# One list for all 48 weight-sum steps of the second FFN, two chains alternating, drawn on from the first FFN's last third

## The chip, the cores and the metric

The kernel runs on one core of a Trainium2 chip. The metric is the device time of one execution in microseconds, lower is better. Three executions of the kernel before took 1138.20, 1135.95 and 1139.35 us, with a median of 1138.2 us. For this kernel a difference under about 0.3% (3.4 us) cannot be told from no change.

## The reference

One decoder layer over 512 tokens of width 1024, in float32. Two feed-forward blocks (FFN, hidden width 2816) stand around a pair of parallel token mixers:

```python
h = x
h = h + 0.5 * swiglu(rmsnorm(h, norm_ffn1), ffn1_gate, ffn1_up, ffn1_down)
u = rmsnorm(h, norm_mix)
parts = split(u @ w_in)                       # queries, keys, values, gates of both mixers
o_a = native_sparse_attention(...)            # compressed + selected blocks + window of 512
o_b = sliding_window_attention(...)           # window of 128, with sinks
merged = sigmoid(ga) * (o_a @ w_branch_a) + sigmoid(gb) * (o_b @ w_branch_b)
h = h + merged @ w_out
h = h + 0.5 * swiglu(rmsnorm(h, norm_ffn2), ffn2_gate, ffn2_up, ffn2_down)
out = rmsnorm(h, norm_final)

def swiglu(x, w_gate, w_up, w_down):
    return (silu(x @ w_gate) * (x @ w_up)) @ w_down
```

## The kernel before, in words

**Products.** Every float32 weight block and every operand is split into a high and a low part, and a product is made of three matmuls (high x high, high x low, low x high). One weight block is 512 KB in most places (128 partitions x 1024 floats). Its way is: SP loads it into one of four `raw` buffers (L143), ACT casts the high part `whi` (L151), DVE subtracts to get the low part `wlo` (L155), and PE uses both. There are four `whi`/`wlo` slots. Casts are issued two blocks ahead of the matmuls that need them, and the load of block n + 4 goes into the buffer that the low part of block n has freed. SP carries these loads in program order.

**Fewer products by weight sums.** Some stages use a 2 x 2 block scheme with seven products in place of eight. It needs sums and differences of quarters of the weights. These are not made on an engine: POOL issues DMAs from HBM to HBM, of two kinds, a plain copy into a scratch tensor and an accumulating one that adds to it (`issue`, L396 to L401: L399 accumulates, L401 copies). A weight sum is a chain of eight such steps over four scratch tensors, where most steps need the one or two before them in the same chain to have landed, and POOL waits for that in its own queue before it issues the step. The first FFN has its own sums (`unit_sums`, tensors `s_...`, 32 steps of 512 KB; lines L478 and L480), for the tiles 8 to 15 of its hidden width ("unit" stage, matmuls at L791).

**The 48 steps of the second FFN**, 1 MB each, are six chains of eight:

- four chains from `four_steps(f)` for f = 0, 8, 12, 17 (`FOURS`): scratch tensors named `w`. Each serves 14 weight blocks (`raw<-w` and quarters of gate and up) of a tile group of four (function `four`, matmuls at L1883, 14 blocks of 12 matmuls each).
- two chains from `down_sums(f0)` for f0 = 0, 8: scratch tensors named `t`. They serve the first and the second down projection (function `down`).

The order in which the second FFN uses them: tiles 4, 5, then `four` 0, tiles 6, 7, first `down`; `four` 8, `four` 12, tile 16, second `down`; `four` 17, tile 21, and the last down projection.

**Who draws a step, before.** Three generators hold the 48 steps, and a `next(...)` written at some place of the program emits one step into POOL's queue at that place:

- `in_mixers` holds 24 steps, three chains in turn (`four` 0, `four` 8, `down` 0). `Schedule.follow` draws them at 24 places of the mixers' instruction list `ORDER`, which is written out by hand.
- `in_merge` holds the 8 steps of `four` 12, drawn at every second turn of the merge's two loops over d (the gated merge and the product with `w_out`).
- `in_ffn2` holds 16 steps, first the 8 of `down` 8, then the 8 of `four` 17, one chain after the other. They are drawn at places inside the second FFN.

A place in the program is only a place in POOL's queue. POOL issues a step as soon as what stands ahead of it in its queue is done and the step's own predecessors have landed, whatever PE does then.

**What else stands in POOL's queue** near these steps: in the first FFN's last third and in the merge, the running sum of squares `sqacc` for the next norm (L673); in the mixers low parts (L155), rotations (L1186, L1265) and the weighing of probabilities (L1582, L1584); in the merge the product of a stored gate with the norm's factor (`z<-z,r_b`, L1750).

Of the kernel before, what the change touches and what calls it, by code (L numbers as in the profile page):

```python
# [362 lines left out]
def layer(ctx, tc, a, out):  # L363
# [33 lines left out]
    def issue(o, i, add):  # L397
        if add:
            gpsimd.dma_start(o, i, accum_op=OP.add)  # L399
        else:  # L400
            gpsimd.dma_start(o, i)  # L401

    def down_sums(f0):

        def part(j, k):
            return dram(a["ffn2_down"], (f0 + j) * 128 * D + k * 512, [[D, 128], [256 * D, 4], [1, 512]])

        t = [t_sums[f0, k] for k in range(4)]
        return [(t[0], part(0, 1), 0), (t[2], part(0, 1), 0), (t[0], part(0, 0), 1), (t[2], part(1, 1), 1),
                (t[1], t[0], 0), (t[1], part(1, 1), 1), (t[3], t[1], 0), (t[3], part(1, 0), 1)]  # L410
# [3 lines left out]
    def four_steps(f):  # L414

        g0, g1, u0, u1 = (dram(a[f"ffn2_{what}"], kh * 512 * DFF + f * 128, [[DFF, 512], [1, 512]])
                          for what in ("gate", "up") for kh in range(2))
        t1, t3, t2, t4 = (four_sums[f, m] for m in (5, 7, 6, 4))
        return [(t1, g0, 0), (t3, u0, 0), (t1, u0, 1), (t3, u1, 1), (t2, t1, 0), (t2, u1, 1), (t4, t2, 0), (t4, g1, 1)]

    def in_mixers():

        x = [y for z in zip(four_steps(FOURS[0]), four_steps(FOURS[1]), down_sums(0)) for y in z]
        for y in x:
            issue(*y)
            yield

    def in_merge():

        for y in four_steps(FOURS[2]):  # L430
            issue(*y)
            yield

    def in_ffn2():

        for y in down_sums(8) + four_steps(FOURS[3]):
            issue(*y)
            yield

    def four_block(f, m, kk):  # L440

# [374 lines left out]
    def ffn(after, begun, side, sums, early):  # L816


        norm = {}

        def col():
            norm["col"] = col_of(sums)

        def rows():
            norm_rows(norm["col"])
            for j, b in enumerate(begun):
                swiglu(*b, j)

        lo, hi = UNITS[1]
        adds = unit_sums(1)  # L830
        for third, (f0, f1) in enumerate(THIRDS):
            f = f0 + (len(begun) if f0 == 0 else 0)
            while f < f1:
                if lo <= f < hi:
                    if f == lo:
                        W.full, W.more_bufs = len(W.raw) - 1, 0
                    unit(f - f0)
                    f += 2
                    if f > lo + 2:
                        next(early, None)  # L840
                    continue
                first = f == len(begun)
                pg = acc(False)
                mm3(pg, W.next(), u_in, KD, col if first else None)
                pu = acc(False)
                mm3(pu, W.next(), u_in, KD, rows if first else None)
                swiglu(pg, pu, f - f0)
                f += 1
                if third == 0:
                    if f == 8:  # L850
                        sums_of_u(0, 0)
                    next(side, None)
                    for _ in range(6):
                        next(adds, None)
                else:
                    next(early, None)
                    next(side, None)
            settle(later)
            settle(owed)
            for d in range(KD):  # L860
                po = acc(False)
                mm3(po, W.next(), g_in, f1 - f0)
                if third == 2 and d < KD - 1:
                    W.prep(W.pos + W.AHEAD)
                vector.scalar_tensor_tensor(h[:, d], po, 0.5, h[:, d], op0=OP.mult, op1=OP.add)
                if third == 0:
                    if d < 3:
                        sums_of_u(0, d + 1)
                    next(side, None)
                if third == 1 and d in (0, 2, 4, 6, 7):  # L870
                    next(early, None)
                if third == 2:
                    after(d)
        for g in (adds, side, early):
            for _ in g:
                pass
# [128 lines left out]
    with ExitStack() as mixing:  # L1005
# [693 lines left out]
        nsa_count, swa_turns = [0], []  # L1699
        attend([*swa_units(0), *swa_units(1), *nsa_units(0), *nsa_units(1, (3, 2, 1, 0))])  # L1700
        plan.clock["sp"] = plan.clock["store"] = 0.0
        plan.follow(ORDER, in_mixers())
        W.pos = pos[0]
        W.prepped = pos[0] + 2
        att_stack.close()
# [33 lines left out]
                stt(p[:, 1], y[:, :256], -1.0, p[:, 0], op0=OP.mult, op1=OP.subtract)  # L1739
            split(four_hi[:, k, 2 * second:2 * second + 2], four_lo[:, k, 2 * second:2 * second + 2], p)  # L1740

        merge_steps = in_merge()

        with pool("merge", 2, side="right") as mp:
            mh, ml = (mp.tile([128, KD, S], F32R, name=n, bufs=1) for n in ("mh", "ml"))

            def load_z(d):
                z = mp.tile([128, S], F32, name="z%d" % (d // KD))
                nc.sync.dma_start(z, zd[d])
                gpsimd.tensor_tensor(z, z, r_b, op=OP.mult)  # L1750
                return z

            za, zb = load_z(0), None
            for d in range(KD):
                nc.sync.dma_start(h[:, d], hd[d])
                gates_z = [za, zb]
                if d + 1 < KD:
                    za = load_z(d + 1)
                if d not in GB_EARLY:
                    gates_z[1] = mp.tile([128, S], F32, name="z1")  # L1760
                    ps = acc(False)
                    mm3(ps, W.next(), u_in, KD)
                    vector.tensor_tensor(gates_z[1], ps, r_b, op=OP.mult)
                if d + 1 in GB_EARLY:
                    zb = load_z(KD + d + 1)
                for z, x in zip(gates_z[::-1], (b_in, a_in)):
                    scalar.activation(z, z, AF.Sigmoid)
                    ps = acc(False)
                    mm3(ps.rearrange("p (t c) -> p t c", t=4), W.next(), x, 4)
                    vector.tensor_tensor(z, z, ps, op=OP.mult)  # L1770
                y, z = gates_z
                vector.tensor_tensor(y, y, z, op=OP.add)
                split(mh[:, d], ml[:, d], y)
                if d % 2 == 0:
                    next(merge_steps, None)

            m_in = (lambda k: mh[:, k]), (lambda k: ml[:, k])
            for d in range(KD):
                ps = acc(False)
                mm3(ps, W.next(), m_in, KD)  # L1780
                vector.tensor_tensor(h[:, d], ps, h[:, d], op=OP.add)
                norm_in(d, 2)
                for i in {4: (0, 1), 5: (2,), 6: (3,)}.get(d, ()):
                    sums_of_tokens(i, mp, ("z0", "z1"))
                if d % 2:
                    next(merge_steps, None)


    with pool("temp3", 2) as temp, pool("end") as end:
# [175 lines left out]
                for n in range(4):  # L1965
                    turns.append(lambda n=n: whole(n))

        turns, steps = [], in_ffn2()

        def turn_back():  # L1970
            if turns:
# [192 lines left out]
```

## Time and profile before

| | |
|---|---|
| median of three runs | 1138.2 us |
| the profiled execution | 1138.66 us |
| its span, first to last instruction | 1136.9 us |
| PE busy | 1096.1 us (96%) |
| DVE, ACT, POOL busy | 757.9, 541.5, 218.8 us |
| moved by POOL's DMA queue (q0) | 67.11 MB in 26176 packets |
| moved by SP's DMA queue (q1) | 159.98 MB in 172696 packets |

The stages, by the start of their matmuls: first FFN up to 366 us (unit stage 143 to 224 us), mixers up to about 640 us, merge and `w_out` up to 748 us, second FFN to the end. A row of the windows view gives, for a stretch of time, each engine's busy time with its count of instructions, the granted TensorE clock (1.00 is full), the mean busy share of the 16 DMA engines and the rate. In a timeline row the square bracket holds the idle time of the engine before the instruction and what ended it.

### The profile page before, as it was taken

How to read it: one execution, taken by the hardware profiler on the slowest of the kernel's cores; microseconds unless marked ns; L12 is line 12 of the kernel's file. 1: busy time of each engine (PE TensorE's matmuls, PEld its weight loads, DVE VectorE, ACT ScalarE, POOL GpSimd, SP SyncE). 2: the span in 40 equal slices, each digit the busy share in tenths (PEclk: the TensorE clock that was granted, in tenths of full speed). 3: DMA queues.
4: the chain of work that ended last, by engine and by line, in shares of the span. 5: the costliest groups of instructions: out<-in, count | busy, mean ns of one | idle time of the engine just before them, and what ended most of it. 6: DMA issues, size and time to landing. Idle time of an engine off the chain costs nothing.

```text
span 1136.9 us, 15814 instructions
## 1 busy us (share of the span) xinstructions
PE 1096.1 (96%) x5827; PEld 938.9 (83%) x5827; DVE 757.9 (67%) x1358; ACT 541.5 (48%) x988; POOL 218.8 (19%) x253
## 2 busy tenths in 40 slices
PE   9999999999999998999999999977959999999987
PEld 7888899988888998998888888866748888888876
DVE  5656777854556588987777376554647876787653
ACT  5433344432344466767677434435434446554432
POOL 0211210000003145744345322221100000000002
PEclk9999999999999999999999999989989999999999
DMA  6988979788756365359897879669996565646612
GB/s 210 260 214 211 241 186 263 228 286 259 246 179 176 86 186 161 116 170 262 268 236 253 217 239 259 170 157 264 297 257 194 193 196 167 187 148 196 212 56 75
DMA packets 201414, 232.44 MB, mean 204 GB/s; under 512 B 7924, under 2 KB 152120, under 8 KB 201016
## 3 DMA queue, kind: packets, MB, share of 16 engines
q1 hardware_dynamic: 172696, 159.98, 44.4%
q0 software_dynamic: 26176, 67.11, 25.6%
q10 hardware_dynamic: 2464, 4.33, 1.0%
q8 instruction: 46, 0.75, 0.3%
q14 instruction: 32, 0.26, 0.1%
HBM read 211.47 MB, written 87.03 MB: 263 GB/s over the span
## 4 chain that ended last, share of the span: by engine, by line
PE 82%; DVE 8%; DMA 4%; ACT 3%; issue 2%; POOL 0%; POOLq 0%; ACTq 0%; DVEq 0%; SPq 0%
PE acc L387 27%; PE o L387 19%; PE s L387 18%; PE o L791 3%; PE o L1883 3%; PE acc L1883 2%; PE s L1883 2%; DMA raw<-in_ffn_up_dram 2%; PE tp L1647 2%; PE s L791 2%; PE acc L791 2%; DVE wlo L155 2%; ACT whi L151 1%; DMA raw<-in_ffn_gate_dram 1%; PE tp L387 1%
## 5 line engine op out<-in xcount | busy, mean ns | idle before, releaser
L155 DVE TENSOR_TENSOR wlo<-raw,whi 128x1024 fp32r<-128x1024 f32 (+2 forms) x225 | 260.8, 1179 | 86.2 <-ACT whi L151 84.3
L151 ACT CAST whi<-raw 128x1024 fp32r<-128x1024 f32 (+2 forms) x250 | 228.7, 938 | 135.8 <-PE acc L387 23.6
L387 PE MATMUL acc<-uh,whi 128*128 128x512 f32 x224 | 92.6, 413 | 4.6 <-ACT whi L151 4.6
L387 PE MATMUL acc<-uh,wlo 128*128 128x512 f32 x224 | 89.9, 401 | 0.0
L387 PE MATMUL acc<-ul,whi 128*128 128x512 f32 x224 | 89.7, 400 | 0.0
L387 PE MATMUL acc<-whi,uh 128*128 128x256 f32 x224 | 65.8, 294 | 1.2 <-ACT whi L151 1.2
L387 PE MATMUL acc<-wlo,uh 128*128 128x256 f32 x224 | 63.6, 284 | 0.1
L387 PE MATMUL acc<-whi,ul 128*128 128x256 f32 x224 | 63.5, 284 | 0.0
L1662 DVE TENSOR_TENSOR pts<-tp,pts 128x512 fp32r<-128x512 f32 (+1 forms) x62 | 41.9, 686 | 22.7 <-ACT pts L1659 22.1
L2061 POOL TENSOR_TENSOR o_t<-o_t,g_b 128x512 f32<-128x512 f32 (+1 forms) x5 | 5.9, 1179 | 252.7 <-ACT z L2055 252.7
L387 PEld LDWEIGHTS acc<-uh,whi 128*128 128x128 f32 x224 | 43.3, 193 | 12.4 <-ACT whi L151 5.0
L387 PEld LDWEIGHTS acc<-uh,wlo 128*128 128x128 f32 x224 | 43.3, 193 | 10.7 <-DVE wlo L155 1.2
L1561 ACT ACTIVATE pbuf<-s,m 128x256 f32<-128x256 f32 (+3 forms) x96 | 47.5, 503 | 8.4 <-DVE c L1571 4.1
L387 PE MATMUL acc<-G,whi 128*128 128x512 f32 x164 | 50.5, 389 | 0.0
L387 PEld LDWEIGHTS acc<-ul,whi 128*128 128x128 f32 x224 | 43.3, 194 | 7.6
L387 PE MATMUL s<-G,whi 128*128 128x512 f32 x160 | 49.3, 390 | 0.0
L387 PE MATMUL o<-G,whi 128*128 128x512 f32 x156 | 48.3, 390 | 0.4 <-DVE G L776 0.4
L387 PE MATMUL o<-uh,whi 128*128 128x512 f32 x120 | 48.4, 404 | 0.0
L1659 ACT CAST pts<-tp 128x512 fp32r<-128x512 f32 (+1 forms) x62 | 35.5, 586 | 24.9 <-PE tp L1647 19.2
L387 PE MATMUL o<-ul,whi 128*128 128x512 f32 x120 | 47.2, 394 | 0.0
L387 PE MATMUL o<-uh,wlo 128*128 128x512 f32 x120 | 47.0, 392 | 0.0
L1584 POOL TENSOR_SCALAR pbuf<-pbuf,c,gate 128x256 f32<-128x256 f32 (+3 forms) x57 | 35.3, 629 | 57.6 <-DVE c L1571 36.7
(471 smaller groups left out, 3023.8 us busy)
## 6 DMA issues: line engine op xcount, KB each, us to landing
raw<-in_ffn_gate_dram SPq DMA_DIRECT2D x42, 512.0 KB, 6.0
raw<-in_ffn_down_dram SPq DMA_DIRECT2D x34, 512.0 KB, 5.4
w<-in_ffn_up_dram POOLq DMA_DIRECT2D x16, 1024.0 KB, 10.8
raw<-w SPq DMA_DIRECT2D x32, 512.0 KB, 4.4
raw<-in_ffn_up_dram SPq DMA_DIRECT2D x30, 512.0 KB, 6.0
t<-in_ffn_down_dram POOLq DMA_DIRECT2D x12, 1024.0 KB, 10.8
raw<-in_w_in_dram SPq DMA_DIRECT2D x20, 512.0 KB, 4.7
raw<-s SPq DMA_DIRECT2D x16, 512.0 KB, 5.0
```

Source lines behind the costliest of these rows:

```text
L151: self.nc.scalar.copy(self.place(i)[0][:, k0:k1], self.raw[i][:, k0:k1])
L155: engine.tensor_tensor(lo, self.raw[i][:, k0:k1], f32(hi), op=OP.subtract)
L387: tensor.matmul(out, lhsT, rhs, start=start, stop=stop)
L791: tensor.matmul(o, a_[:, n], x(k), start=new and n == step == 0, stop=n == 7 and step == 2, skip_group_check=True)
L1561: scalar.activation(u.p[:, hd], b.view[:, j], AF.Exp, bias=u.m[:, hd:hd + 1], scale=-1.0, accum_out=u.sum[:, hd:hd + 1])
L1584: e.tensor_scalar(u.p[:, hd], u.p[:, hd], u.c[:, hd:hd + 1], u.gate[:, hd:hd + 1], op0=OP.mult, op1=OP.mult)
L1647: tensor.transpose(ps[:w, hd], u.p[:, hd, kb * w:kb * w + w], ident)
L1659: scalar.copy(p.hi, flat(b.ps)[:w])
L1662: vector.tensor_tensor(p.lo, flat(b.ps)[:w], f32(p.hi), op=OP.subtract)
L1883: tensor.matmul(ps, x, y[:, k], start=new and kk == k == step == 0, stop=kk == k == 1 and step == 2, skip_group_check=True)
L2061: gpsimd.tensor_tensor(y, y, left["g_b"][:, cs], op=OP.mult)
```

## The change

The three generators become one, `sum_steps`, that holds all 48 steps as three pairs of chains. Within a pair the two chains alternate step by step: `four` 0 with `down` 0, then `four` 8 with `four` 12, then `down` 8 with `four` 17. It is drawn on at more places: four times after tiles of the first FFN's last third, three times in that third's down projection (after d = 1, 3, 5), at the mixers' 24 places as before, three times in the `w_out` loop of the merge (d = 1, 3, 5) in place of eight times over both loops, and at the second FFN's places, which are unchanged. So before the second FFN 34 steps are issued in place of 32, and 14 are left in place of 16. No instruction is added or taken away on any engine; PE, DVE, ACT and SP keep their order.

```diff
-    def in_mixers():
-        x = [y for z in zip(four_steps(FOURS[0]), four_steps(FOURS[1]), down_sums(0)) for y in z]
-        for y in x:
-            issue(*y)
-            yield
-    def in_merge():
-        for y in four_steps(FOURS[2]):
-            issue(*y)
-            yield
-    def in_ffn2():
-        for y in down_sums(8) + four_steps(FOURS[3]):
-            issue(*y)
-            yield
+    def sum_steps():
+        for pair in ((four_steps(FOURS[0]), down_sums(0)), (four_steps(FOURS[1]), four_steps(FOURS[2])),
+                     (down_sums(8), four_steps(FOURS[3]))):
+            for both_steps in zip(*pair):
+                for y in both_steps:
+                    issue(*y)
+                    yield
+
+    steps = sum_steps()
...
                     next(early, None)
                     next(side, None)
+                    if f > 18:
+                        next(steps, None)
...
                 if third == 2:
                     after(d)
+                    if d in (1, 3, 5):
+                        next(steps, None)
...
-        plan.follow(ORDER, in_mixers())
+        plan.follow(ORDER, steps)
...
-                if d % 2 == 0:
-                    next(merge_steps, None)
...
-                if d % 2:
-                    next(merge_steps, None)
+                if d in (1, 3, 5):
+                    next(steps, None)
...
-        turns, steps = [], in_ffn2()
+        turns = []
```

Line numbers after the removed lines are lower by four to eight in the changed kernel. In the rows below `s_14_...` are the last sums of the first FFN; `w_5_87`, `w_7_88` are two scratch tensors of `four` 0, `w_4_98` the last of `four` 12, `w_5_99`, `w_7_100` the first two of `four` 17; `t_0_79`, `t_0_81` belong to `down` 0 and `t_8_83` to `t_8_86` to `down` 8. A source `in_ffn_...` is a weight in HBM.

POOL's queue from the first FFN's last own sum to the norm behind its down projection, before:

```order
L480 DMA s_14_4_118<-s_14_2_116 16x8192
L478 DMA s_14_4_118<-in_ffn_gate_dram 512x256
L673 TENSOR_TENSOR sqacc<-sqacc,z 128x512 x7
L1024 MEMSET turn_b 64x512
L686 TENSOR_TENSOR ny<-nv,mhalf 128x4
```

The same stretch of POOL's queue now:

```order
L470 DMA s_14_4_118<-in_ffn_gate_dram 512x256
L401 DMA w_5_87<-in_ffn_gate_dram 512x512
L401 DMA t_0_79<-in_ffn_down_dram 512x1x512
L401 DMA w_7_88<-in_ffn_up_dram 512x512
L401 DMA t_0_81<-in_ffn_down_dram 512x1x512
L665 TENSOR_TENSOR sqacc<-sqacc,z 128x512
L399 DMA w_5_87<-in_ffn_up_dram 512x512
L665 TENSOR_TENSOR sqacc<-sqacc,z 128x512 x2
L399 DMA t_0_79<-in_ffn_down_dram 512x1x512
L665 TENSOR_TENSOR sqacc<-sqacc,z 128x512 x2
L399 DMA w_7_88<-in_ffn_up_dram 512x512
```

Four copies have moved directly behind the last own sum of the first FFN, with nothing between them, and three accumulating steps between the additions of `sqacc`.

POOL's queue from the merge's last additions into the second FFN, before:

```order
L399 DMA w_4_98<-in_ffn_gate_dram 512x512
L686 TENSOR_TENSOR ny<-nv,mhalf 128x4
L401 DMA t_8_83<-in_ffn_down_dram 512x1x512
L401 DMA t_8_85<-in_ffn_down_dram 512x1x512
L399 DMA t_8_83<-in_ffn_down_dram 512x1x512
L399 DMA t_8_85<-in_ffn_down_dram 512x1x512
L401 DMA t_8_84<-t_8_83 16x16384
L399 DMA t_8_84<-in_ffn_down_dram 512x1x512
L401 DMA t_8_86<-t_8_84 16x16384
L399 DMA t_8_86<-in_ffn_down_dram 512x1x512
L401 DMA w_5_99<-in_ffn_gate_dram 512x512
L401 DMA w_7_100<-in_ffn_up_dram 512x512
```

The same place now:

```order
L401 DMA w_5_99<-in_ffn_gate_dram 512x512
L665 TENSOR_TENSOR sqacc<-sqacc,turn_a 128x512 x2
L678 TENSOR_TENSOR ny<-nv,mhalf 128x4
L401 DMA t_8_85<-in_ffn_down_dram 512x1x512
L401 DMA w_7_100<-in_ffn_up_dram 512x512
L399 DMA t_8_83<-in_ffn_down_dram 512x1x512
L399 DMA w_5_99<-in_ffn_up_dram 512x512
L399 DMA t_8_85<-in_ffn_down_dram 512x1x512
L399 DMA w_7_100<-in_ffn_up_dram 512x512
L401 DMA t_8_84<-t_8_83 16x16384
L401 DMA w_6_101<-w_5_99 16x16384
L399 DMA t_8_84<-in_ffn_down_dram 512x1x512
```

The first copy of each of the two last chains has moved ahead of the norm, and the two chains now alternate where they stood one behind the other.

More of the change, by code (lines that the diff above doesn't have):

```diff
@@ L1740, in sums_of_tokens @@
             split(four_hi[:, k, 2 * second:2 * second + 2], four_lo[:, k, 2 * second:2 * second + 2], p)
-        merge_steps = in_merge()
         with pool("merge", 2, side="right") as mp:
```

## The prediction

> **What bounds the kernel now.** I read the page first, then PE's waits, the windows, and the timelines of PE, ACT and POOL at the waits.
>
> ```profile
> span 1136.9 us, 15814 instructions
> PE 1096.1 (96%) x5827; PEld 938.9 (83%) x5827; DVE 757.9 (67%) x1358; ACT 541.5 (48%) x988; POOL 218.8 (19%) x253
> PE   9999999999999998999999999977959999999987
> ```
>
> PE is the bound: 1096.1 of 1136.9 us busy. The change leaves every matmul in place, so it can win only from the 41 us of idle PE and from stretches with a low granted clock; it can lose anywhere. PE's slices have their one deep dip at three quarters of the span (7, 7, then 5). PE's waits say what lies there:
>
> ```profile
> PE tp L387 <- POOL sqacc L673: 5.8, 1, 5.8
> PE acc L387 <- ACT whi L151: 5.8, 2, 4.6
> PE tp L1919 <- ACT G L1930: 5.5, 1, 5.5
> PE acc L1883 <- DVE t L1823: 5.5, 1, 5.5
> ```
>
> The columns are microseconds in all, times, longest. The windows (time, PE, PEld, DVE, ACT, POOL busy, clock, DMA share, GB/s) place them:
>
> ```profile
> 184.00:222.00 38.00, 38.00 (x319) 38.00 (x319) 31.81 (x39) 18.97 (x23) 1.03 (x1) 1.00 0.78 226
> 340.00:366.00 26.00, 26.00 (x117) 21.56 (x116) 17.23 (x19) 12.24 (x18) 7.25 (x6) 1.00 0.65 186
> 400.00:456.00 56.00, 52.05 (x420) 50.48 (x419) 49.06 (x125) 33.96 (x91) 27.20 (x24) 0.97 0.61 183
> 640.00:748.00 108.00, 108.00 (x478) 89.44 (x477) 65.93 (x85) 46.66 (x72) 28.43 (x24) 1.00 0.79 225
> 748.00:760.00 12.00, 6.16 (x28) 5.12 (x27) 7.86 (x10) 5.93 (x8) 3.51 (x3) 0.76 0.36 91
> 760.00:800.00 40.00, 33.22 (x146) 26.30 (x146) 20.23 (x39) 18.74 (x28) 7.16 (x8) 0.90 1.00 254
> 800.00:834.00 34.00, 32.60 (x142) 25.94 (x140) 17.68 (x19) 11.63 (x13) 4.58 (x5) 1.00 0.99 286
> 834.00:868.00 34.00, 23.80 (x92) 18.82 (x92) 20.04 (x30) 14.26 (x20) 3.05 (x4) 0.80 0.90 237
> ```
>
> The merge (640 to 748) has PE busy throughout. The norm behind it (748 to 760) waits for ACT and the sums of squares, with DMA at 0.36: no weight sum is in that. In the second FFN's first third DMA is full (1.00, 0.99, 0.90), and PE loses most where `four` 0 ends and tile 6 begins:
>
> ```profile
> 837.59 1.04 ACT L151 CAST whi<-raw 128x1024 fp32r<-128x1024 f32 x1 [7.31 <-DMA raw<-in_ffn_gate_dram]
> 838.68 0.80 PE L387 MATMUL acc<-uh,whi 128*128 128x512 f32 x1 [4.56 <-ACT whi L151]
> 844.35 1.05 ACT L151 CAST whi<-raw 128x1024 fp32r<-128x1024 f32 x1 [5.72 <-DMA raw<-in_ffn_up_dram]
> 851.62 2.33 PE L1919 MATMUL tp<-ident,t 128*128 128x128 f32 x8 [5.48 <-ACT G L1930]
> ```
>
> Tile 6's first cast waits 7.31 us for its load, and PE waits 4.56 behind it. The next cast waits 5.72 for the next load; ACT works in order, so the work that `four` 0's results need (`G`) stands behind this cast and PE waits 5.48 more. Thus 10.0 us of idle PE are a DMA matter. The low clock adds to it: 92 matmuls at the merge's 108.00/478 = 0.226 us would take 20.8, they took 23.80, so 3.0 more. 13.0 us are the most that the change can reach. The fourth wait in the list ends on DVE, not on a load, and stays.
>
> **The change, part by part.** Four copies go to POOL's queue behind the last sum of the first FFN. The code draws them after later tiles, but POOL's next work is 158 us away:
>
> ```profile
> 184.40 1.03 POOL L478 DMA_DIRECT2D s<-in_ffn_gate_dram  x1 [4.23 <-DMA s<-s]
> 343.67 1.33 POOL L673 TENSOR_TENSOR sqacc<-sqacc,z 128x512 f32<-128x512 f32 x1 [158.23 <-ACT z L672]
> ```
>
> They need nothing that is computed, so they issue at 185 to 189 us, one about every 1.03 us, in the unit stage: 4 MB beside the loads. There loads land thus (first row), and in the second FFN, with sums beside them, thus (second row, 799 to 842 us):
>
> ```profile
> DMA to landing us min/median/max: 3.7/4.6/5.4
> DMA to landing us min/median/max: 5.5/11.1/17.2
> ```
>
> The unit stage runs 319 matmuls in 38.00 us, 24 to a block, so 2.86 us a block. Four buffers turn round in one landing plus one cast (1.05) and one `wlo` (1.22): (11.1 + 2.3)/4 = 3.35 us a block at the median, 0.5 too slow; (17.2 + 2.3)/4 = 4.9 at worst, 2.0 too slow. Four sums at 5 to 6 us each hold the queue for some 22 us, 7 blocks: 7 x 0.5 = 3.5, and with 4 blocks at the worst pace 8. Against it stands a cushion: casts run two blocks ahead, and this cast, in the same stage, waited 2.97 us for its load while PE ran on (38.00 of 38.00):
>
> ```profile
> 193.23 1.05 ACT L151 CAST whi<-raw 128x1024 fp32r<-128x1024 f32 x1 [2.97 <-DMA raw<-in_ffn_up_dram]
> ```
>
> With a cushion of about 3 us, 3.5 is nearly covered: I take +1 (0 to +3.5; +8 without a cushion).
>
> Three accumulating steps stand between the additions of `sqacc`, 345 to 365 us. Each costs POOL about 1 us of issue between additions 4 us apart; PE there is full and DMA at 0.65. Cover: the pause between additions. Gone, it would delay the norm by 1 us. I take 0 (0 to +1).
>
> Mixers: the 24 places hold 12 accumulating steps as before, 4 copies and 8 scratch-to-scratch steps in place of 6 and 6. By the merge's DMA list, prices are close:
>
> ```profile
> w<-in_ffn_up_dram POOLq DMA_DIRECT2D x4, 1024.0 KB, 9.2
> w<-in_ffn_gate_dram POOLq DMA_DIRECT2D x1, 1024.0 KB, 5.3
> w<-w POOLq DMA_DIRECT2D x2, 5.3
> ```
>
> A step now needs the one two places before it, not three. The tightest pair of places:
>
> ```profile
> 582.55 1.19 POOL L399 DMA_DIRECT2D t<-in_ffn_down_dram  x1
> 594.16 0.55 POOL L401 DMA_DIRECT2D w<-w  x1
> ```
>
> There an accumulating step will wait for a scratch copy issued 11.6 us before it; at 5.3 that has landed, and POOL does not stop (behind it in POOL's queue stand `pbuf` weighings, for which PE would wait). At 401 us an accumulating step (9.2) stands where a copy (6.7) did, and the chain that sets the end runs there through a load, with PE at 52.05 of 56.00:
>
> ```profile
> w<-in_ffn_gate_dram POOLq DMA_DIRECT2D x2, 1024.0 KB, 6.7
> 406.04 5.40 DMA raw<-in_cmp_k_w_dram
> ```
>
> The 2.5 us of longer sum lie over that load's start; a load shares rather than waits, so I take +0.5 (0 to +2.5), and nothing for the other places (-1.5 to +1.5).
>
> Merge: three steps in place of eight. PE is full there (108.00 of 108.00), so nothing is won; the norm's 5.8 us end on ACT's squares and stay. 0.
>
> Second FFN: 14 steps in place of 16, and the merge's last step, which ran into it at 757.87, is gone:
>
> ```profile
> 757.87 1.02 POOL L399 DMA_DIRECT2D w<-in_ffn_gate_dram  x1
> 798.25 0.52 POOL L401 DMA_DIRECT2D t<-t  x1 [8.21 <-DMA t<-in_ffn_down_dram]
> 804.22 1.15 POOL L399 DMA_DIRECT2D t<-in_ffn_down_dram  x1 [5.45 <-DMA t<-t]
> 862.35 1.02 POOL L399 DMA_DIRECT2D w<-in_ffn_gate_dram  x1 [5.19 <-DMA w<-w]
> 811.30 10.34 DMA raw<-in_ffn_gate_dram
> 824.09 20.19 DMA raw<-in_ffn_up_dram
> q0 software_dynamic: 5968, 17.83, 64.2%
> q1 hardware_dynamic: 9098, 12.34, 30.9%
> ```
>
> Seven steps ran from 757.87 to 798.25 (5.8 us each, one chain that waits for itself: the bracket), eight from 804.22 to 862.35 (7.3 each). Fourteen from 761 at 5.8 to 7.3 end at 842 to 863; I take 850, where before it was about 871. Two alternating chains leave fewer gaps in POOL's queue, so the loads of `four` 0 (two stand in the chain of waits, 10.34 and 20.19 us long) share with more sums, but the sums end 20 us sooner. By tile 6's gate at 838.68 thirteen steps had landed before; now 12 to 14 will have. The loads that tile 6 needs therefore see about the same bytes ahead of them: the first wait stays (-1 to +1 of it), the second loses what the queue's earlier end gives. I put that at 2 of 5.48 us: -2. Bounds: all 13.0 us vanish but some 2 of joining: -11; or all fourteen sums land ahead of tile 6's loads, one scratch step (5.3) more: +5.
>
> On this place the Trainium skill has a rule, "DMA: Bandwidth & Descriptors", section "Queues, rings and completion order": a DMA engine goes round between the queue rows that have work, a packet from each. By the q0 and q1 rows above (757 to 875 us) a packet held 2988 bytes on q0 and 1356 on q1. With both always filled, SP would get 1356/4344 = 31% of 254 GB/s, 79 GB/s or 6.6 us a block, where 12.34 MB in 118 us were 5.0 us a block. By the rule, keeping POOL's queue filled costs SP more than the sums' count says: 14 blocks at 1.6 us are 22 us less what the sums' end near 844 gives back, so `four` 0 would end some 6 later and the second wait would go: FFN2 at 0 to +3, the total near 1141. The trace's 64.2% against 30.9% agrees in kind, but holds one chain, so it cannot decide.
>
> **Sum.** +1 + 0 + 0.5 + 0 - 2 = -0.5, made against the profiled execution's 1138.66 us (span 1136.9): 1138.2 there. That execution lies 0.46 above the median 1138.2, so 1137.7 against the median.
>
> **Rivals.** (1) Faster: two chains run at the pace of gapless queues; if a step takes 5.8 us or less, the fourteen end by 842, the two waits at tile 6 shrink to a join of 2 and the clock stays up: -11 + 1.5 = -9.5, near 1129. For it: 20 us less of sums; against it: 286 GB/s at a DMA share of 0.99 already in `four` 0, so faster sums are slower loads.
>
> (2) Slower, in `four` 0: with POOL's queue always filled, the loads of its 14 blocks give way to all fourteen sums; from 0.4 us a block later (14 x 0.4 = 5.6) it decides. FFN2 +5, total 1138.2 + 1.5 + 5 = about 1144.5. For it: the 20.19 us load. Against: the same bytes are then gone for tile 6.
>
> (3) Slower, in the unit stage: the four copies at 185 us take loads from 2.86 to 3.35 us a block and the cushion of 3 us is less than it looks, since casts already wait 2.97: +5 to +8, total about 1144. It decides when landings pass 4 x 2.86 - 2.3 = 9.1 us for more than six blocks.
>
> (4) The change does not do what its places say: the copies do not wait for the last third. That is part of the forecast.
>
> **Chances.** Forecast, within 1134 to 1142: 0.42; rival 1: 0.30; rival 2 0.13; rival 3 0.15. The likeliest case's own range is 1134 to 1142. The whole range reaches from rival 1 (1129) to the two slower ones with the mixers' upper bound (1146); beyond stand rival 1 with all 13 us below, and 2 with 3 together above. A difference under 0.3%, 3.4 us, cannot be told from no change: faster (below 1134.8) 0.30 and a little of the forecast, 0.33; slower (above 1141.6) 0.28; same 0.39.
>
> **What would show it.** Four copies at 185 to 189 in POOL's timeline, with PE idle under 2 us in 184 to 222 (right), or 5 or more (rival 3). PE at 26.00 and 108.00 still in 340 to 366 and in the merge. In the second FFN the last sum issued at about 843 to 850; PE's first wait at tile 6 near 4.5, the second near 3.5. Rival 1 shows both below 2 and DMA below 0.9 from 842 on; rival 2 more idle inside `four` 0 and its end past 838. I am wrong altogether if a PE wait appears in the mixers on POOL's `pbuf` or on a load beside a sum: there the new order was priced at half a microsecond.

## The result and the profile after

The changed kernel takes 1150.8 us (median of 4, 1150.5 to 1151.2) against 1138.1 before: 1.1% slower, ratio 1.0114 with an interval of 1.0096 to 1.0131. The profiled execution has a span of 1148.8 us against 1136.9, that is 11.9 us more. It was forecast at 1137.7, within 1129 to 1146.

The stretches below are those of the prediction's windows, each shifted by as much as the kernel has fallen behind there, with the end of the first FFN (347 to 414) besides (columns as before: time, PE, PEld, DVE, ACT, POOL busy, clock, DMA share, GB/s). Windows of the changed kernel:

```profile
184.00:222.00 38.00, 34.15 (x261) 33.63 (x260) 26.33 (x32) 16.36 (x20) 0.00 (x0) 0.91 0.86 284
347.00:373.00 26.00, 26.00 (x117) 21.56 (x116) 16.88 (x19) 12.25 (x18) 10.72 (x9) 1.00 1.00 239
373.00:391.00 18.00, 11.54 (x93) 11.13 (x92) 5.24 (x13) 4.68 (x7) 3.08 (x4) 0.96 0.73 182
391.00:414.00 23.00, 23.00 (x175) 23.00 (x175) 12.00 (x38) 10.18 (x23) 3.02 (x4) 0.88 0.22 62
656.00:764.00 108.00, 108.00 (x478) 89.42 (x477) 64.60 (x85) 46.79 (x73) 26.12 (x20) 1.00 0.62 182
777.00:817.00 40.00, 33.53 (x145) 26.48 (x144) 20.38 (x38) 18.86 (x29) 8.56 (x10) 0.85 1.01 259
817.00:851.00 34.00, 29.19 (x121) 21.95 (x120) 16.35 (x18) 9.28 (x10) 4.29 (x5) 1.00 1.07 287
851.00:885.00 34.00, 30.23 (x128) 23.36 (x128) 22.98 (x32) 17.42 (x24) 0.00 (x0) 0.95 0.60 165
```

The unit stage, full before (38.00), now has 261 matmuls in place of 319 in its 38 us. In the first FFN's last down projection (347 to 373) PE is full, but DMA has gone from 0.65 to 1.00. Behind it stands a new hole (11.54 of 18) and a slow clock (0.88). The merge is full as before: fewer steps there won nothing. In the second FFN, `four` 0 (817 to 851) is emptier than before (29.19 of 34 against 32.60) and tile 6 behind it fuller (30.23 against 23.80). PE's longest waits say the same: two at tile 6 have gone, one has come at the first FFN's end:

```profile
PE tp L387 <- DVE sqacc L690: 6.0, 1, 6.0
PE tp L387 <- POOL sqacc L665: 5.8, 1, 5.8
PE acc L1875 <- DVE t L1815: 5.5, 1, 5.5
```

To place the loss I took the start of the same DVE instruction in both traces (all 1358 stand in the same order) and subtracted. Microseconds behind the kernel before, for the instructions that start at the time in the head in the kernel before:

| kernel | 170 | 230 | 345 | 380 | 420 | 450 | 800 | 819 | 836 | 880 | 1090 |
|---|---|---|---|---|---|---|---|---|---|---|---|
| changed | -0.1 | 7.0 | 7.0 | 14.2 | 17.7 | 16.2 | 16.9 | 23.0 | 19.7 | 13.3 | 11.8 |

So: unit stage +7.0; norm behind the first FFN +7.2; front of the mixers +2.0; the rest of mixers, merge and norm +0.7; second FFN from 800 us on -5.1 (16.9 to 11.8), with 6 lost in `four` 0 and 10 won at tile 6. The sum is 11.8. Each of these profiles is one execution, and the one of the kernel before (1138.66 us) lies above the medians that it had later; so the columns say where time goes, and the medians how much. How far one profile can be trusted is seen in two kernels below, e2 and e3, which are the kernel before up to the merge: at 450 us they stand at -2.0 and 0.0.

**The unit stage.** POOL's timeline, ACT's casts, PE's gap and the windows around it, changed kernel:

```profile
175.45 1.05 POOL L401 DMA_DIRECT2D w<-in_ffn_gate_dram  x1
176.09 1.21 POOL L401 DMA_DIRECT2D t<-in_ffn_down_dram  x1
176.72 1.21 POOL L401 DMA_DIRECT2D w<-in_ffn_up_dram  x1
177.36 1.33 POOL L401 DMA_DIRECT2D t<-in_ffn_down_dram  x1
...
189.74 1.05 ACT L151 CAST whi<-raw 128x1024 fp32r<-128x1024 f32 x1 [2.80 <-DMA raw<-in_ffn_gate_dram]
197.10 1.04 ACT L151 CAST whi<-raw 128x1024 fp32r<-128x1024 f32 x1 [6.30 <-DMA raw<-s]
201.14 1.05 ACT L151 CAST whi<-raw 128x1024 fp32r<-128x1024 f32 x1 [3.00 <-DMA raw<-s]
...
198.19 0.39 PE L783 MATMUL o<-bhi,whi 128*128 128x256 f32 x1 [3.19 <-ACT whi L151]
199.45 0.58 PE L783 MATMUL o<-bhi,wlo 128*128 128x256 f32 x1 [0.65 <-DVE wlo L155]
195.00:199.00 4.00, 0.61 (x2) 0.30 (x2) 0.83 (x1) 1.04 (x1) 0.00 (x0) 0.93 1.08 361
199.00:205.00 6.00, 5.55 (x26) 5.55 (x27) 3.77 (x5) 3.01 (x4) 0.00 (x0) 0.50 0.77 255
```

The four copies are issued within 2 us. Of the three loads issued behind them, the first two land 13.0 and 16.7 us later. The third keeps SP busy with its issue alone for 9.81 us, where the kernel before needed 0.36, and since SP works in order the next load goes out only at 193.06 (first row before, second row now):

```profile
183.24 0.36 SPq L143 DMA_DIRECT2D raw<-s  x1
183.16 9.81 SPq L143 DMA_DIRECT2D raw<-s  x1
```

The casts run dry, and PE stands for 3.8 us (3.19 and 0.65) around 197. It then runs at a clock of 0.50 to 205, which costs about 3 more (26 matmuls in 6 us, where 319 in 38 us would make it 3.1). The queues in 182 to 194 us (packets, MB, share), and the landing times of the loads (the view has a landing for two of the three, so its median is their middle):

```profile
q0 software_dynamic: 906, 3.42, 78.5%
q1 hardware_dynamic: 901, 0.91, 24.1%
DMA to landing us min/median/max: 13.0/14.9/16.7
```

The packets are equal in number, 906 and 901, and a packet of a copy holds 3.8 KB against 1.0 KB of a load: SP gets 0.91 MB in 12 us, 76 GB/s, while POOL's queue gets 285.

**The norm.** POOL, ACT, DVE and PE at the end of the first FFN, changed kernel:

```profile
368.76 1.03 POOL L399 DMA_DIRECT2D w<-in_ffn_up_dram  x1
375.12 1.29 POOL L665 TENSOR_TENSOR sqacc<-sqacc,z 128x512 f32<-128x512 f32 x1 [1.91 <-ACT z L664]
382.74 0.52 POOL L1020 MEMSET turn_b<- 64x512 f32 x1 [6.32 <-DMA hd<-h]
383.30 0.40 ACT L1021 CAST vc<-turn_b 64x256 fp32r<-64x256 f32 x1 [8.32 <-POOL turn_b L1020]
384.76 1.99 ACT L151 CAST whi<-raw 128x1024 fp32r<-128x1024 f32 x2
385.84 2.36 DVE L155 TENSOR_TENSOR wlo<-raw,whi 128x1024 fp32r<-128x1024 f32 x2 [10.60 <-ACT whi L151]
388.12 0.15 DVE L676 TENSOR_SCALAR nv<-tp 128x4 f32<-128x4 f32 x1
390.63 2.07 PE L387 MATMUL tp<-sqacc,ones 128*128 128x128 f32 x8 [6.03 <-DVE sqacc L690]
```

The same three instructions in the kernel before, of POOL, ACT and DVE:

```profile
369.48 0.52 POOL L1024 MEMSET turn_b<- 64x512 f32 x1
370.03 0.40 ACT L1025 CAST vc<-turn_b 64x256 fp32r<-64x256 f32 x1 [2.05 <-POOL turn_b L1024]
372.57 2.36 DVE L155 TENSOR_TENSOR wlo<-raw,whi 128x1024 fp32r<-128x1024 f32 x2 [4.33 <-ACT whi L151]
```

The chain is read downwards. The last addition of `sqacc` still waits for ACT's `z`, so POOL is not late with it. `turn_b` takes over memory that `h` held, so POOL's MEMSET waits until the last store of `h` to HBM (`hd<-h`) has landed. ACT works in order: `vc` waits for `turn_b`, and the two casts stand behind `vc`. DVE's two `wlo` wait for the casts, `nv` of the norm stands behind them, and PE waits 6.03 us for what comes of `nv`. The same store landed in 2.2 us before and takes 8.1 now (before in 340 to 375, after in 347 to 385; each a median of the three stores of seven whose landing the trace holds, 2.0 to 2.5 and 7.0 to 11.4 us). The last store, on which MEMSET waits, is issued at 374.24, 8.5 us before MEMSET starts:

```profile
hd<-h SPq DMA_DIRECT2D x7, 256.0 KB, 2.2
hd<-h SPq DMA_DIRECT2D x7, 256.0 KB, 8.1
```

**The second FFN.** The last sum, and the two waits at tile 6 that were 4.56 and 5.48 us before:

```profile
841.17 1.02 POOL L399 DMA_DIRECT2D w<-in_ffn_gate_dram  x1 [3.45 <-DMA w<-w]
858.41 0.50 PE L387 MATMUL acc<-uh,whi 128*128 128x512 f32 x1 [1.35 <-ACT whi L151]
867.06 0.30 PE L1911 MATMUL tp<-ident,t 128*128 128x128 f32 x1 [0.90 <-ACT G L1922]
```

The kernel is 17 to 23 us late there. The fourteen sums run from 777.37 to 841.17, 4.9 us a step, and both waits are nearly gone.

### The profile page after: what moved, and what is told of

Read it like the earlier page. It is cut to its first block, busy times and chain, and to the rows that moved or that the text cites. A ratio compares the mean times of both kernels' runs of the same rounds, so it can differ in the third digit from the quotient of the medians.

```text
span 1148.8 us, 15814 instructions
## 1 busy us (share of the span) xinstructions
PE 1100.0 (96%) x5827; PEld 940.4 (82%) x5827; DVE 757.2 (66%) x1358; ACT 541.2 (47%) x988; POOL 219.7 (19%) x253
## 4 chain that ended last, share of the span: by engine, by line
PE 81%; DVE 7%; DMA 6%; ACT 3%; issue 2%; POOL 0%; POOLq 0%; ACTq 0%; DVEq 0%; SPq 0%
PE acc L387 26%; PE o L387 18%; PE s L387 17%; PE o L1875 3%; PE acc L1875 3%; PE s L1875 3%; PE o L783 2%; PE tp L1643 2%; DMA raw<-in_ffn_gate_dram 2%; DVE wlo L155 2%; PE s L783 2%; PE acc L783 2%; DMA raw<-s 1%; ACT whi L151 1%; DMA raw<-in_ffn_up_dram 1%
```

## The experiments

Medians; "less before" is the difference to the kernel before as it ran beside that kernel, where it had medians of 1134.1 to 1138.1. The other columns are as in the table above. a1, b1, c1 and d1 start from the changed kernel. g1, h1, i1, k1, f1 and e1 start from d1, and the lines printed show what they change beyond it (g1 alone draws at the norm again). e2 and e3 start from the kernel before. Two kernels leave work out: g1 moves a sixteenth of three sums, f1 drops the last two chains.

| kernel | us | less before | 230 | 345 | 380 | 450 | 800 | 819 | 880 | 1090 |
|---|---|---|---|---|---|---|---|---|---|---|
| changed | 1150.8 | +12.7 | 7.0 | 7.0 | 14.2 | 16.2 | 16.9 | 23.0 | 13.3 | 11.8 |
| a1_copies_held | 1145.8 | +9.3 | -0.9 | -0.9 | 6.1 | 9.1 | 8.8 | 13.7 | 7.9 | 6.3 |
| b1_none_at_norm | 1146.0 | +9.5 | 5.0 | 5.0 | 5.0 | 7.7 | 7.7 | 12.7 | 6.9 | 5.4 |
| c1_order_alone | 1140.9 | +4.4 | -0.4 | -0.4 | -0.4 | -2.3 | -2.9 | 1.8 | 0.2 | 0.2 |
| d1_both_mended | 1139.1 | +2.7 | -0.4 | -0.4 | -0.4 | 2.1 | 1.5 | 7.9 | 0.5 | 0.5 |
| g1_small_at_norm | 1137.0 | +1.5 | -0.8 | -0.8 | -0.8 | 2.3 | 2.2 | 7.3 | -0.6 | -0.6 |
| h1_two_in_unit | 1139.6 | +4.1 | -0.6 | -0.6 | -0.6 | 1.5 | 1.7 | 6.3 | -1.2 | -1.3 |
| i1_one_after_other | 1135.3 | -0.2 | -0.8 | -0.8 | -0.8 | 2.8 | 2.8 | 6.6 | -2.3 | -2.7 |
| k1_late_first_step | 1135.0 | -1.9 | -1.0 | -1.0 | -1.0 | -1.0 | -1.4 | 2.3 | -3.6 | -3.9 |
| f1_no_sums_ffn2 | 1123.4 | -12.1 | -1.0 | -1.0 | -1.0 | 1.0 | 1.3 | -1.4 | -15.5 | -15.5 |
| e1_held_in_ffn2 | 1127.2 | -6.9 | -0.8 | -0.8 | -0.8 | 2.9 | 2.5 | -0.1 | -14.2 | -11.9 |
| e2_before_held | 1126.2 | -8.0 | -0.7 | -0.7 | -0.7 | -2.0 | -2.0 | -4.7 | -18.8 | -5.7 |
| e3_before_held_spaced | 1122.4 | -14.4 | 0.1 | 0.1 | 0.1 | 0.0 | -0.1 | -2.8 | -16.9 | -16.6 |

### The copies in the unit stage, and the steps at the norm

Copies held until their tile is done (a1):

```diff
                     if f > 18:
+                        gpsimd.tensor_copy(pad, f32(G[:, 7 + f - f0, 0:4]))
                         next(steps, None)
```

> The changed kernel with the four copies held on POOL until the gate values of tiles 18 to 21 exist (a 4-column POOL copy that reads them stands ahead of each). Theory: the copies, issued at 175 to 178 us into the unit stage, cost the 7.0 us by which the kernel falls behind there; held to about 300 to 335 us, where PE is full and DMA has room, they cost nothing: 1150.8 - 7.0 = 1143.8 us, PE 38 of 38 in 184 to 222, the norm's 6.0 us wait unchanged. Rival, 4 MB beside loads cost the same wherever they run: about 1150.

Steps at the norm moved to the merge (b1), and both edits together (d1):

```diff
                     after(d)
-                    if d in (1, 3, 5):
-                        next(steps, None)
...
-                if d in (1, 3, 5):
+                if d < 6:
                     next(steps, None)
```

> The changed kernel with the three accumulating steps not drawn in the first FFN's last down projection; the w_out loop draws six steps in place of three. Theory: these three sums delay the loads of w_in ahead of the mixers; the low part of one such block stands in DVE's queue ahead of the norm's nv, so PE waits 6.0 us there and runs 3.3 us worth of slow clock behind it: 1150.8 - 9.6 = 1141.2 us, the unit stage still 7 behind. Rival, the wait at the norm comes from the loads that the unit stage has already put late, whatever POOL does: 1150.

> The changed kernel with the four copies held until tiles 18 to 21 are done, and the three accumulating steps of the first FFN drawn in the merge. Theory: both losses (7.0 and 9.6) go and the second FFN's gain of 4.7 stays: 1150.8 - 16.6 = 1134.2 us. Rival, the losses move on, since the bytes must be moved beside loads somewhere: 1138 or more.

Each edit removed the loss at its place and left the other. In a1 the copies went out at 303, 315, 325 and 336 us, and PE stayed full:

```profile
302.92 0.66 POOL L401 DMA_DIRECT2D w<-in_ffn_gate_dram  x1
336.35 0.72 POOL L401 DMA_DIRECT2D t<-in_ffn_down_dram  x1
300.00:340.00 40.00, 40.00 (x179) 33.11 (x178) 23.23 (x29) 15.96 (x21) 4.95 (x8) 1.00 0.87 276
```

The same 4 MB cost 7.0 us (5.0 in b1) in one place and nothing in another. In b1 the 7.2 at the norm are gone. The totals fell by less than expected, by 5.0 and 4.8, since the second FFN gave back only about 2.4 in these kernels; in b1 the expectation had also counted the front of the mixers as won, and it kept 2.7. d1 has neither loss and still is 2.7 above the kernel before, 4.9 more than expected: the mixers' front keeps its 2.5, and the second FFN's gain was 1.0 in that profile, not the 4.7 that I had put there. The rival's number (1138 or more) came out, its mechanism did not: the front loses no more in d1 than in a1 (3.0) or b1 (2.7), so no loss has moved there.

### Bytes or issue, and how much the buffers carry

```diff
+                    small[0] = True          # g1: issue() moves a sixteenth of the rows
                     if d in (1, 3, 5):
                         next(steps, None)
+                    small[0] = False
```

> The kernel with the four copies held until tiles 18 to 21, and the three accumulating steps back between the additions of sqacc, but each moving only a sixteenth of its rows (15/16 of these three sums are left out). Theory, it is their bytes, beside the loads of w_in and the stores of hd, that make the wait at the norm: with 0.2 MB in place of 3 MB it is gone, as when no step is drawn there: 1139 us, DVE's wlo at 372 no later than 1 us. Rival, it is POOL's time to issue them between the additions: 1146 as with whole steps there.

It is the bytes: with the three issues in place and 0.2 MB moved, nothing is lost at 380 (-0.8), and the stores `hd<-h` land in 2.3 us again.

```diff
-                        gpsimd.tensor_copy(pad, f32(G[:, 7 + f - f0, 0:4]))
+                        if f > 20:           # h1: two copies free, two held
+                            gpsimd.tensor_copy(pad, f32(G[:, 7 + f - f0, 0:4]))
```

> No step at the norm; two of the four copies (the first of each chain) free to issue at about 174 us in the unit stage, the other two held until tiles 20 and 21. Four free copies cost 5 to 7 us there, none cost 0. Theory, the loads behind get only some 75 GB/s until the copies are through (about 10 us for two), and buffers filled ahead carry some 8 us of that: 0 to 1 us, so 1139 to 1140 us. Rival, each copy costs its share: 3 us, 1142.

Two copies cost nothing by 230 us (-0.6), four cost 5 to 7. That rests on one profile, of h1's fastest execution (1137.4); its median is 1139.6, as expected. The loads beside the copies in h1 were late too (landings of two of them), but the buffers filled ahead lasted:

```profile
DMA to landing us min/median/max: 10.8/11.9/13.0
```

### The mixers' front

```diff
-            if n % 64 == 63 if n < 512 else n % 38 == 37:
+            if n > 63 and (n % 64 == 63 if n < 512 else n % 38 == 37):
```

> The kernel with both losses mended, with no step drawn at the mixers' first place (401 us; each step moves one place on, the merge draws seven). Theory, an accumulating step at 401 and the one at 415 delay the first loads of the mixers by 2 to 3 us in every run that has the new list ahead of them; without the one at 401 the mixers run at most 1 us behind the kernel before at 415 us: 1137 us. Rival, the delay at 410 does not come from that step: 2 to 3 us behind as before, 1139.

k1 is 1.0 ahead at 450 where d1 is 2.1 behind. The accumulating step at 401 us costs some 3 us there; the kernel before has a copy at that place, and so has c1, which loses nothing. Over all profiles: the nine kernels with that step lose 2.0 to 3.7 us from 380 to 450, and c1, e2, e3 and k1, without it, between -1.9 and 0. In d1 the load `raw<-in_cmp_k_w_dram` beside it takes 7.51 us where it took 5.40, and PE waits 2.35 us behind it.

### Order, number and place of the steps in the second FFN

```diff
-                    if f > 18:
-                        next(steps, None)
...
+                if d in (2, 6):              # c1: the merge's first loop, besides six in the second
+                    next(steps, None)
...
+                if third == 0 and n < 2:     # and two more in the second FFN
+                    next(steps, None)
```

> The new list of three pairs of chains, at numbers of steps as before the change: none in the first FFN, 24 in the mixers, 8 in the merge, 16 in the second FFN. Theory: no loss ahead of the second FFN (0 behind the kernel before at 800 us, within 1.5), so the new order of the list is not what made the kernel slower. In the second FFN the changed kernel won 4.7 us: if alternating the two chains did that, about 1133; if the two steps fewer did it, about 1138. Rival, the mixers' new order costs the 3 us seen at 385 to 410: 1141.

c1 lost nothing ahead of the second FFN, so the list's order is not what made the change slow. Its time is that of the rival (1141), but the loss is not in the mixers, where the rival had it. In the second FFN sixteen alternating steps lost 3.1 us (-2.9 to 0.2) against the kernel before with sixteen in single file.

```diff
+        last = down_sums(8), four_steps(FOURS[3])
...
+            serial = pair[0] is last[0]          # i1
-            for both_steps in zip(*pair):
+            for both_steps in pair if serial else zip(*pair):
```

> The kernel with both losses mended, the last two chains one behind the other in place of alternating (14 steps from the second FFN's start on, as with alternation). Theory, alternation keeps POOL's queue filled: it slows four 0 by some 6 us and gives that back at tile 6; one chain at a time slows four 0 less and leaves the waits at tile 6: within 2 us of 1139. Rival, the order is worth 3 us or more, one way or the other.

In i1 fourteen steps in single file won 5.5 us there (2.8 to -2.7), more than expected. Alternating, the changed kernel won 5.1, and a1, b1, d1, g1, h1 and k1 won 1.0 to 3.0. So by these profiles two steps fewer are worth some 4 to 8 us, and alternation takes 0.4 to 4.5 of them back. That alternation costs is likely and not shown: the changed kernel's 5.1 is nearly i1's, and though by medians i1 stands 2.9 better than d1 (-0.2 against +2.7), the intervals of their ratios, 0.9985 to 1.0021 and 1.0003 to 1.0036, overlap a little.

```diff
+    t_sums.update({(8, k): t_sums[0, k] for k in range(4)})
+    four_sums.update({(FOURS[3], m): four_sums[FOURS[0], m] for m in (5, 7, 6, 4)})
...
-                if d in (1, 3, 5):
+                if d < 4:
...
-        turns = []
+        turns, steps = [], iter(())          # f1
```

> The kernel with both losses mended, and no sum at all drawn from the second FFN's start on: the steps of the last two chains are left out (their loads read the finished sums of the first two). Theory, all waits on loads from four 0 to tile 6 and the slow clock behind them come from the 14 sums: some 9 us less than with them, 1130 us, and that is what there is to win in the second FFN. Rival, other waits (DVE's t, the join at tile 6) take their place: 1135 or more.

f1 leaves out all 16 steps of the last two chains, 14 of which d1 has in the second FFN. They cost 14.8 us by medians (+2.7 to -12.1), where some 9 were expected, and more than the 13.0 that the prediction had as the most to be won. What is left of DMA's load in tiles 4 and 5 is little, which shows where there is room (f1, 760 to 800 us, then d1 in the same stretch):

```profile
760.00:800.00 40.00, 33.81 (x149) 27.20 (x149) 19.07 (x39) 17.45 (x26) 1.04 (x1) 0.88 0.16 53
760.00:800.00 40.00, 33.93 (x148) 27.79 (x149) 20.08 (x39) 17.81 (x27) 8.04 (x10) 0.85 1.01 256
```

PE is as busy in the one as in the other: sums that run and end there are free. Those that run on into `four` 0 are not. So the next kernels hold the later steps (the changed places in `four` and `down` are not printed):

```diff
+        def draw(n, hold=True):
+            if hold:
+                k = held[0]
+                held[0] += 1
+                vector.memset(stops[:, 0, k:k + 1], 0.0)
+                gpsimd.tensor_copy(stops[:, 1, k:k + 1], stops[:, 0, k:k + 1])
+            for _ in range(n):
+                next(steps, None)
...
-                next(steps, None)            # behind a tile of the second FFN; e1
+                draw(*{4: (2, False), 5: (2, False), 6: (2, True), 7: (2, True)}.get(f, (0, False)))
```

> The kernel with both losses mended and the last two chains one behind the other; in the second FFN the first four steps stay free, and each later step is held on POOL until DVE has come to its place (a one-column fill on DVE that a POOL copy reads): two behind tile 6, two behind tile 7, two in the first down projection, two each in four 8 and four 12. None runs in four 0. Theory, the 14 sums cost some 12 to 16 us where they meet the loads of four 0 and tile 6, and the time from tile 6 on (DMA at 0.55 from 868 us) carries them for nothing: most of the loss of sums in the second FFN is won, 1126 us (1123 to 1130). Rival, sums cost the loads the same wherever they run in it: 1135.

> The kernel before the change, its order and its 24, 8 and 16 steps, with the second FFN's steps from the fifth on held in the same way (two more in the first down projection). Theory, not how many steps are left for the second FFN but where they run in it sets the cost: 16 held steps are as good as 14, 1126 us (1123 to 1130). Rival, moving steps ahead of the second FFN is what pays: some 2 to 4 us above the other kernel of this call.

Both came out as expected, e1 at 1127.2 and e2 at 1126.2, ratios 0.9932 (0.991 to 0.9953) and 0.9929 (0.9903 to 0.9955). Both have the last two chains in single file; with the steps held, sixteen left for the second FFN do as well as fourteen, so there the place sets the cost and not the number. Alternating chains were not tried with held steps. e2's profile is that of its slowest execution (1133.0); it shows 12 us given back between 880 and 960, where two copies and two accumulating steps stood close together. Its other executions took 1124.4 to 1127.0, so most of these 12 us are not in them.

> The kernel before the change with the second FFN's steps held, one step further: the first two copies of down 8 are drawn in the merge (ten steps there), and the held steps stand singly (two behind tile 6, one behind tile 7, two in the first down projection, two each in four 8 and four 12, one behind tile 16), since the profile of the other held kernel showed two copies and two accumulating steps close together at 878 to 900 us and PE falling back there. Theory: without that fall, and with nothing of the merge's chain run into the norm, 1124 us (1122 to 1127); 1123.4 was the kernel with no sum in the second FFN at all. Rival, the held steps still meet loads in the first down projection, whatever their spacing: 1127 or more.

```diff
-                if d % 2 == 0:
+                if d % 2 == 0 or d == 7:     # e3: ten steps in the merge
                     next(merge_steps, None)
...
-                if d % 2:
+                if d in (1, 3, 4, 5, 6):
                     next(merge_steps, None)
```

e3, with single held steps, is at 1122.4: ratio 0.9884 (0.9865 to 0.9903) to the kernel before, the fastest kernel here and within 2 us of f1, which has no sum in the second FFN. Its windows from `four` 0 on, with the last one in the kernel before as a fourth row:

```profile
800.00:834.00 34.00, 34.00 (x156) 28.22 (x154) 22.38 (x25) 15.13 (x18) 0.00 (x0) 1.00 0.68 208
834.00:868.00 34.00, 33.73 (x154) 27.67 (x153) 26.39 (x40) 18.04 (x25) 4.46 (x5) 1.00 0.57 165
868.00:958.00 90.00, 90.00 (x405) 74.09 (x403) 69.08 (x91) 42.62 (x50) 6.06 (x10) 1.00 0.82 253
868.00:958.00 90.00, 90.00 (x405) 74.35 (x405) 64.96 (x78) 41.37 (x49) 0.00 (x0) 1.00 0.58 186
```

PE is full but for 0.27 us; DMA has gone up from 0.58 to 0.82 behind tile 6, and PE does not feel it. How much of e3's gain over e2 is the spacing and how much the two copies in the merge was not tried apart.

## Why the prediction was wrong

**Unit stage: forecast +1 (up to 3.5, 8 without a cushion), measured +7.0.** That the copies do not wait for the last third was right, they went even earlier (175 us), and they held the queue for 23 us (the last lands at 198.6 us) where 22 were forecast. The step that failed is the size of the landing times, and so the cushion. It took the median of 11.1 us from the second FFN, where one chain waits for itself and leaves gaps, and where the view has a landing for four loads only, 5.5 to 17.2 us. Four copies without dependences leave no gaps: the loads behind them took 13.0 and 16.7 us, and the third stood 9.81 us in SP's issue, a term that the sum did not have. The cushion is real, but carries two copies (h1), not four. What the cushion does not carry was also priced without the clock: of the 7.0, 3.8 are idle PE and about 3 the clock at 0.50 behind it. Rival 3 gave the mechanism and its price (5 to 8) at a chance of 0.15; its sign, 5 us or more of idle PE, was not reached (3.85), since the clock made up the rest. The Trainium skill's rule in "DMA: Bandwidth & Descriptors", section "Queues, rings and completion order", that an engine takes a packet from each queue row in turn, was weighed for the second FFN only. In the unit stage the trace agrees with it closely (906 packets against 901). That SP's measured 76 GB/s is near the 79 worked out for both queues filled is chance: the queues moved 362 GB/s in place of 254, and SP's share of the bytes was 21% in place of 31%.

**Norm: forecast 0 (0 to +1), measured +7.2, and a slow clock behind it.** This step failed outright, and no rival had it. It named POOL's pause between additions as the cover and looked at POOL and PE alone. The additions were on time; the 3 MB were not costed as traffic, though DMA had only 0.35 of room, and it went to 1.00. What hangs on that traffic is a store, `hd<-h`, whose landing frees memory that POOL fills next, and three engines queue in order behind it.

**Mixers: forecast +0.5 (0 to +2.5), measured +2.0 here and 2.5 in d1**, the upper end. d1 shows the mechanism as named, one accumulating step at 401 us and the load beside it (7.51 against 5.40 us). The +2.0 of the changed kernel cannot be put down to that alone: it also holds the slow clock behind the norm, 175 matmuls in 23 us where the kernel before has 196 (375 to 398), some 2.5 us. No stop of POOL appeared at the tightest pair, as forecast.

**Merge: forecast 0, measured 0.**

**Second FFN: forecast -2 (-11 to +5), measured -5.1, and -1.0 to -3.0 in the six other kernels with fourteen alternating steps.** The number is inside its bounds, the way to it was another. The forecast had the fourteen steps at 5.8 to 7.3 us each, the last one issued 82 to 89 us after the first, the first wait at tile 6 near 4.5 and the second near 3.5. The steps took 4.9, the last was issued after 64 us, and the waits were 1.35 and 0.90: that is rival 1's mechanism. Rival 2's came with it, since the loads of `four` 0 lost 6 us to the alternating chains; tile 6 gave 10 back. That both together come out near the forecast is luck. In the six other kernels the first wait stays at 3.3 to 4.6 and the second is at most 1.5, which is nearer to what was forecast. The 13.0 us taken as the most to be reached were too few: in f1's profile the second FFN is 16.8 us shorter than before (1.3 to -15.5). Most of this was to be had by holding the steps, not by drawing them elsewhere.

## What to carry to other kernels

A DMA step moved to an earlier place in a queue that nothing holds runs when the queue is free, not where the program has it; price it by what loads and stores run at that moment, and hold it with a tiny dependent instruction if they matter. Before calling a stretch free, ask of each load and store in it who waits for its landing, the reuse of its buffer included, and what stands behind that waiter on an engine that works in order. A few large transfers without dependences between them starve small-packet loads until they are through; buffers filled ahead carry a certain number of them and no more, so here their spacing mattered more than their number.

## What the runs showed of the hardware

- Two DMA queues with work shared by packets, 906 to 901 in 12 us, and so by bytes as 3.42 to 0.91 MB: a queue with packets of 1.0 KB had 76 GB/s beside one with packets of 3.8 KB. The issue of one load on SP then took 9.81 us in place of 0.36.
- A PE gap of 3.8 us, 3.19 of them in one piece, was followed by 6 us at a granted clock of 0.50. The Trainium skill's "TensorE: Matmul & The Clock Gate", section "Part 1: The HAM clock gate (the "warmup" mystery)", has idle of some 3.4 us halve the clock; the trace agrees in this place, to within 0.2 us. In b1, with the same four copies, PE stood 3.9 us in four pieces of 0.64 to 1.78 us, and the clock stayed at 1.00 from 184 to 222. At the norm, 6.03 us of idle were followed by a mean clock of 0.88 over 23 us.
- The first FFN's own sums, with the same instructions ahead of them, did not end at one time: the last was issued at 184.4 us in the profile before, at 188.0 and 189.2 in f1 and k1, and at 172.0 to 175.9 in the eleven others. The prediction's time for the copies was 10 us late for that alone; why they differ was not found.
